# A split-precision encoder layer on one core: TensorE in program order, two weight columns together, weight rests last

## The chip, the core and the metric

The kernel runs on one core of a Trainium2 chip. The metric is the device time of one execution in microseconds (us). TensorE (PE in the profile) multiplies, VectorE (DVE) and ScalarE (ACT) do the elementwise work, GpSimd (POOL) and SyncE (SP) mainly issue transfers. Each engine executes its own instructions in the order in which they stand in its program, and waits on semaphores for the others. The kernel is written with a scheduler: the source gives the operations, and the scheduler chooses the order of each engine's program from what depends on what, priorities and its own estimate of durations, except where the source says otherwise.

## The reference

A residual trunk of two layers over 256 tokens of width 2048, in float32:

```python
for l in range(DEPTH):                      # DEPTH = 2
    h = rms_norm(x, pre_mix_norm[l])
    m = hybrid_mixer(h, l, w_in[l], w_o[l], ...)
    x = x + rms_norm(m, post_mix_norm[l])
    h = rms_norm(x, pre_ffn_norm[l])
    f = (silu(h @ w_gate) * (h @ w_up)) @ w_down
    x = x + rms_norm(f, post_ffn_norm[l])
```

`hybrid_mixer` multiplies `h` by `w_in` (2048 x 6144), feeds eight heads of stick-breaking attention and eight of differential attention with the parts, normalizes each head's output and multiplies by `w_o` (2048 x 2048). The gate and up matrices are 2048 x 5632, the down matrix 5632 x 2048. The weights are 470 MB of reading for two layers with all else, and nearly all of the work is matrix products of 256 tokens with them.

## The kernel before

**Products in three parts.** A float32 operand is split into `hi`, rounded to the form that TensorE multiplies at its full rate, and `lo`, the rest. A product is three matmuls: `sh` with `hi`, `sh` with `lo`, and `sl` with `hi`, where `sh` and `sl` are the rounded form and the rest of the activations, and the stationary operand is a 128 x 128 block of them (128 features by the 128 tokens of one token tile) and the moving operand 128 x 512 of weights. `product` (L1113) issues the three for one bank of PSUM, at L1116, L1117 and L1118. `unit` (L592) does the same for the attention output, at L601 to L603, and `down` (L1353) for the down projection, at L1365, L1366 and L1368.

**Tiles.** 256 tokens are two token tiles (`NT`). 2048 features are 16 tiles of 128 (`KT`), taken two at a time: a pair `kp` of them is one block of weights, 128 partitions x 2 x 512, 512 KB. A stage is a set of columns of 512 weights. Four banks of PSUM hold two columns by two token tiles: in the gate and up stage `c11` and `c12` are gate and up for token tile 0, `c21` and `c22` those for tile 1.

**Weights.** `weight_order` (L77) lays all blocks out in the order of use. SyncE loads each into a `raw` tile (4 of them), ACT rounds it to `hi` (L351), DVE subtracts and writes `lo` (L354); there are six tiles of each, and `feed` (L341) runs four blocks ahead of use (`LOOKAHEAD`). A block's `raw`, `hi` and `lo` come free when the last reader is done.

**Seven products.** For some pairs the 2 x 2 block product (two feature tiles by two columns) is done with seven products instead of eight, from sums of weight blocks (`mixed_weights`, L303: `T` and `G` summed on DVE and POOL, then split into `Th` at L319 and `Tl` at L320) and sums of activations (`token_sums`, L1120, `sh` and `sl`). `seven_products` (L1137) issues them into the four banks and four extra ones, `p1`, `p6`, `p7` and `q5`; `shared_part` combines the extra ones on DVE after the last such pair. In the first gate and up column these are pairs 4 and 6, later more.

**Stages of a layer.** (1) The input projection, six times two columns (`mixer_in`, L980), with the steps of the attention run in between: each call of `tick` (L578) lets waiting parts of the attention issue their next instructions. (2) The output projection: columns 0 and 1 over all pairs, then columns 2 and 3 over `LATE_O` and at the end `LAST_O` = pairs 3 and 7, token tile 0 first for both columns, then tile 1 (L1219 on). `evac_sum` (L614) takes a finished bank out and `rescale` (L626) normalizes: after a chain of small operations (L631 to L636, L508, L509) four instructions of L659 add the scaled columns into `x`. (3) `transposed` (L512) turns 512 columns of `x` at a time on TensorE (L517) into `xT_ps`, and ACT (L520) and DVE (L525) make the rounded form and the rest of the next stage's activations from it (`xF` for the gate and up stage, `xI` for the next layer's input projection), four tiles each time. `inv_rms` (L538) has ACT square all of `x` (L544) for the norm that is applied after the product. (4) Gate and up, eleven columns; in the first one the pairs come as in `FIRST_ORDER` = 0, 1, 3, 2, 7, 4, 6, 5, the first two of them for token tile 0 and then for tile 1. (5) The down projection in two halves of two columns; the last three pairs (`TAIL`) are done column by column within each token tile, so that tile 0 can be rescaled and transposed while tile 1 is still being multiplied. Then the next layer's input projection starts in the same manner as gate and up: two pairs for tile 0, two for tile 1, and the rest.

**What sets the order.** The scheduler orders all engines' programs, PE's too, within what depends on what. `tc.high_priority(offset=URGENT)` lifts some work (evacuation, rescale and, through `then`, tile 1's transposes), `tc.manual_schedule` keeps a block of ACT and DVE work as written (at the end of the output projection), and `tc.issue_after` puts one instruction behind another (`after_rests` and `behind` put sums behind weight rests). Elsewhere PE's order differs from the source locally: where an operand of a seven-product burst is expected late, products of the next pair stand ahead of it.

Of the kernel before, what the change touches and what calls it, by code (L numbers as in the profile page):

```python
# [31 lines left out]
URGENT = 50  # L32
TAIL = 3
# [130 lines left out]
def kernel(  # L164
# [15 lines left out]
    nc = tc.nc  # L180
    const = ctx.enter_context(tc.tile_pool(name="const", bufs=1))
    small = ctx.enter_context(tc.tile_pool(name="small", bufs=4))
    wpool = ctx.enter_context(tc.tile_pool(name="wpool", bufs=1))
    ps = ctx.enter_context(tc.tile_pool(name="ps", bufs=1, space=PSUM))

# [348 lines left out]

    def x_tiles(nm):
        return [x_pool[0].tile([P, 2, S], F32R, tag="xT", bufs=KT, name=f"{nm}_{k}") for k in range(KT)]
# [55 lines left out]
    def unit(accs, stat, i, kp, toks, first, last, ahead=LOOKAHEAD):  # L592
        hi, lo = weights(i, ahead)
        for kk in range(2):
            tick()
            k = 2 * kp + kk
            for t in toks:
                st = stat[k]
                sh, sl = st[:, 0, t * P : (t + 1) * P], st[:, 1, t * P : (t + 1) * P]
                a = accs[t]  # L600
                nc.tensor.matmul(a, sh, hi[:, kk, :], start=first and kk == 0, stop=False, skip_group_check=open_sums[0])  # L601
                nc.tensor.matmul(a, sh, lo[:, kk, :], start=False, stop=False, skip_group_check=open_sums[0])  # L602
                nc.tensor.matmul(a, sl, hi[:, kk, :], start=False, stop=last and kk == 1, skip_group_check=open_sums[0])  # L603
# [22 lines left out]
    def rescale(mg, ssm, t, nm, then=None, newest=None):  # L626
# [11 lines left out]
        if halves:  # L638
# [3 lines left out]
            with tc.issue_after(newest[0].ins):  # L642
                nc.tensor.matmul(xb, ident, first, start=True, stop=False)
# [234 lines left out]

    def opening(pool, accs, xT, stats, sums_of, settle):
# [47 lines left out]
        for kp in range(KT // 2):  # L927
# [3 lines left out]
            if kp + 2 < KT // 2:  # L931
                load()
                fetch(2 * kp + 6)
            for part in ((0,), (1,)) if kp == KT // 2 - 1 else (range(NT),):
                eight_in(accs, xT, 0, PAIRS[0], kp, part, kp == 0, kp == KT // 2 - 1, 0)
# [27 lines left out]
    def eight_in(accs, xT, l, cc, kp, toks, first, last, ahead=LOOKAHEAD):  # L963
        ws = [weights(plan[l]["in"][c, kp], ahead) for c in cc]
        for kk in range(2):
            for t in toks:
                tick()
                st = xT[2 * kp + kk]
                stat = (st[:, 0, t * P : (t + 1) * P], st[:, 1, t * P : (t + 1) * P])
                for col, (hi, lo) in enumerate(ws):  # L970
                    product(accs[2 * t + col], stat, (hi[:, kk, :], lo[:, kk, :]), first and kk == 0, last and kk == 1)
# [8 lines left out]
    def mixer_in(pool, l, rs, xT, mix, mixed):  # L980
# [7 lines left out]
        for n, cc in enumerate(PAIRS):  # L988
# [56 lines left out]
            else:  # L1045
# [3 lines left out]
                for j, kp in enumerate(kps):  # L1049
                    first, last = j == 0, j == len(kps) - 1  # L1050
                    if n == 0 and 2 <= j < 2 + len(IN_SEVEN):
                        sums_of(IN_SEVEN[j - 2])
# [18 lines left out]
                    if n == 0 and j < 2:  # L1071
                        if j == 0:
                            for t in range(NT):
                                for kp in kps[:2]:
                                    eight_in(banks, xT, l, cc, kp, (t,), kp == kps[0], False)
# [34 lines left out]

    open_sums = [False]

    def product(a, stat, moving, first, last):  # L1113
        sh, sl = stat
        hi, lo = moving
        nc.tensor.matmul(a, sh, hi, start=first, stop=False, skip_group_check=open_sums[0])  # L1116
        nc.tensor.matmul(a, sh, lo, start=False, stop=False, skip_group_check=open_sums[0])  # L1117
        nc.tensor.matmul(a, sl, hi, start=False, stop=last, skip_group_check=open_sums[0])  # L1118
# [48 lines left out]
    for l in range(L):  # L1167
# [15 lines left out]
        accs = {(c, t): acc_bank(f"o{l}_{c}_{t}") for c in (0, 1) for t in range(NT)}  # L1183
        forms = {}
        for n, (c, kp) in enumerate(plan[l]["order_o"][:16]):
# [298 lines left out]
```

## Time and profile before

| | |
|---|---|
| median of three runs | 2189.47 us (2189.18 to 2190.63) |
| span of the profiled execution | 2189.2 us |
| TensorE busy | 2174.7 us, 99%, 9980 instructions, granted clock 0.999 |
| weight loads of TensorE busy | 1787.4 us, 82%, 9980 |
| VectorE busy | 1921.7 us, 88%, 2647 instructions |
| ScalarE busy | 1378.0 us, 63% |
| GpSimd busy | 144.2 us, 7% |
| HBM | 470.63 MB read, 223 GB/s over the span |

The profiled execution's own time is within the three runs; its span, from the first to the last instruction, is used as its time below. Rows of the view in order of time begin with the start in us from the start of the span and the duration in us; then come the engine, the line of the kernel, the operation, the output and inputs by name (buffer numbers left out) and their shapes. "x2" joins neighbours of one kind, whose duration is then from the first's start to the last's end. What stands in brackets is how long the engine was idle before and which engine and tile ended that. A duration of a matmul is longer than the step to the next one, since matmuls overlap; steps are read from the starts. Rows of the view of waits give an engine's line, whose result it waited for, the sum of such idle time, how often, and the longest. In the second part of the page each digit is the share in tenths for one fortieth of the span.

### The profile page before, as it was taken

The numbers are of one execution on the slowest core, as the hardware profiler recorded it, in microseconds if no ns is written. First come the engines' busy times: TensorE is split into PE (matmuls) and PEld (weight loads), VectorE is DVE, ScalarE is ACT, GpSimd is POOL, SyncE is SP. The second block draws the span as 40 slices with busy tenths as digits, with TensorE's granted clock in tenths as the row PEclk, the third lists the DMA queues.
The fourth block names the chain that finished last, engine by engine and source line by source line (L and its number), as shares of the span: only waits on it lengthen the run. The fifth ranks groups of instructions, "written<-read, shape, count | busy, mean of one in ns | idle before, by whom it ended". The sixth has DMA issues, their size and how long they took to land.

```text
span 2189.2 us, 28686 instructions
## 1 busy us (share of the span) xinstructions
PE 2174.7 (99%) x9980; PEld 1787.4 (82%) x9980; DVE 1921.7 (88%) x2647; ACT 1378.0 (63%) x2063; POOL 144.2 (7%) x199
## 2 busy tenths in 40 slices
PE   9999999999999999999999999999999999999998
PEld 7888888788888888888878888887788888888886
DVE  7888659999999999989878886699999999999997
ACT  7666665756656666666665656657566566666664
POOL 1100000010010000000010000000000100000000
PEclk9999999999999999999999999999999999999999
DMA  9545577587687786767465555775866877867673
GB/s 322 194 164 173 192 243 267 184 274 234 206 282 235 229 273 210 245 210 257 146 240 173 183 173 183 256 258 195 269 214 226 274 241 232 263 213 234 207 264 101
DMA packets 146033, 489.30 MB, mean 224 GB/s; under 512 B 16592, under 2 KB 17616, under 8 KB 145376
## 3 DMA queue, kind: packets, MB, share of 16 engines
q1 hardware_dynamic: 127712, 450.72, 58.9%
q0 software_dynamic: 17600, 36.22, 8.3%
q8 instruction: 78, 1.28, 0.2%
q10 hardware_dynamic: 576, 0.54, 0.1%
q14 instruction: 67, 0.55, 0.1%
HBM read 470.63 MB, written 16.78 MB: 223 GB/s over the span
## 4 chain that ended last, share of the span: by engine, by line
PE 92%; DVE 5%; ACT 1%; issue 1%; DMA 1%; DVEq 0%; ACTq 0%
PE c L1117 9%; PE c L1118 9%; PE c L1116 9%; PE in L1116 7%; PE in L1118 7%; PE in L1117 7%; PE dn L1368 4%; PE dn L1366 4%; PE dn L1365 4%; PE p L1117 2%; PE p L1118 2%; PE p L1116 2%; PE o L601 2%; PE o L603 2%; PE o L602 2%; DVE lo L354 1%
## 5 line engine op out<-in xcount | busy, mean ns | idle before, releaser
L354 DVE TENSOR_TENSOR lo<-raw,hi 128x1024 fp32r<-128x1024 f32 x514 | 615.2, 1219 | 90.7 <-ACT hi L351 89.8
L351 ACT ACTIVATE hi<-raw 128x1024 fp32r<-128x1024 f32 x514 | 531.3, 1055 | 183.1 <-DMA raw<-in_weights_in_turn_dram 51.3
L1116 PE MATMUL c<-hi,xF 128*128 128x512 f32 x806 | 317.2, 394 | 0.1
L1117 PE MATMUL c<-lo,xF 128*128 128x512 f32 x806 | 314.4, 390 | 1.2 <-DVE lo L354 1.0
L1118 PE MATMUL c<-hi,xF 128*128 128x512 f32 x806 | 314.0, 390 | 0.0
L1117 PEld LDWEIGHTS c<-lo,xF 128*128 128x128 f32 x806 | 151.5, 188 | 33.2 <-DVE lo L354 3.3
L1118 PEld LDWEIGHTS c<-hi,xF 128*128 128x128 f32 x806 | 151.3, 188 | 32.0 <-DVE xF L525 0.4
L1116 PEld LDWEIGHTS c<-hi,xF 128*128 128x128 f32 x806 | 151.4, 188 | 30.3 <-ACT xF L520 0.5
L298 POOL DMA_DIRECT2D T<-in_weights_in_turn_dram x106 | 92.2, 869 | 1257.8 <-DMA T<-in_weights_in_turn_dram 434.6
L1365 PE MATMUL dn<-hi,jh 128*128 128x512 f32 x432 | 168.2, 389 | 0.0
L1366 PE MATMUL dn<-lo,jh 128*128 128x512 f32 x432 | 168.1, 389 | 0.0
L354 DVE TENSOR_TENSOR lo<-G,hi 128x1024 fp32r<-128x1024 f32 x114 | 138.8, 1218 | 21.1 <-ACT hi L351 21.0
L319 ACT ACTIVATE hi<-T 128x1024 fp32r<-128x1024 f32 x114 | 119.7, 1050 | 41.9 <-PE c L1118 23.9
L320 DVE TENSOR_TENSOR lo<-T,hi 128x1024 fp32r<-128x1024 f32 x114 | 138.8, 1217 | 3.2 <-ACT hi L319 2.3
L351 ACT ACTIVATE hi<-G 128x1024 fp32r<-128x1024 f32 x114 | 120.0, 1053 | 30.1 <-PE c L1118 17.4
L319 ACT ACTIVATE Th<-G 128x1024 fp32r<-128x1024 f32 x106 | 111.8, 1055 | 36.8 <-DVE G L335 35.3
L320 DVE TENSOR_TENSOR Tl<-G,Th 128x1024 fp32r<-128x1024 f32 x106 | 129.1, 1218 | 5.5 <-ACT Th L319 5.3
L1368 PE MATMUL dn<-hi,jl 128*128 128x512 f32 x432 | 133.0, 390 | 0.0
L1116 PE MATMUL in<-hi,xT 128*128 128x512 f32 x328 | 131.0, 401 | 1.1 <-ACT hi L921 1.1
L1116 PE MATMUL in<-hi,xI 128*128 128x512 f32 x328 | 131.2, 401 | 0.0
L335 DVE TENSOR_TENSOR G<-G,T 128x1024 f32<-128x1024 f32 x106 | 129.3, 1220 | 1.7
L1117 PE MATMUL in<-lo,xI 128*128 128x512 f32 x328 | 128.1, 390 | 0.3 <-DVE lo L354 0.3
(485 smaller groups left out, 4786.7 us busy)
## 6 DMA issues: line engine op xcount, KB each, us to landing
raw<-in_weights_in_turn_dram SPq DMA_DIRECT2D x514, 512.0 KB, 4.7
G<-in_weights_in_turn_dram SPq DMA_DIRECT2D x114, 512.0 KB, 5.8
T<-in_weights_in_turn_dram SPq DMA_DIRECT2D x106, 512.0 KB, 6.4
T<-in_weights_in_turn_dram POOLq DMA_DIRECT2D x106, 256.0 KB, 7.2
GU<-in_weights_in_turn_dram SPq DMA_DIRECT2D x32, 512.0 KB, 6.5
Gf<-in_weights_in_turn_dram SPq DMA_DIRECT2D x8, 512.0 KB, 6.0
Tf<-in_weights_in_turn_dram SPq DMA_DIRECT2D x8, 512.0 KB, 6.7
V<-in_weights_in_turn_dram SPq DMA_DIRECT2D x8, 512.0 KB, 5.2
```

What stands on the lines that cost most here:

```text
L298: nc.gpsimd.dma_start(sums[i][:, 0, :], stream[i - 1][:, 0, :], accum_op=ALU.add)
L319: nc.scalar.activation(h, w, AF.Copy)
L320: nc.vector.tensor_tensor(out=l, in0=w, in1=h.bitcast(F32), op=ALU.subtract)
L335: nc.vector.tensor_tensor(out=g, in0=g, in1=t2.unsqueeze(1).to_broadcast([P, 2, CW]), op=ALU.add)
L351: nc.scalar.activation(hi, raw, AF.Copy)
L354: rest = nc.vector.tensor_tensor(out=lo, in0=raw, in1=hi.bitcast(F32), op=ALU.subtract)
L1116: nc.tensor.matmul(a, sh, hi, start=first, stop=False, skip_group_check=open_sums[0])
L1117: nc.tensor.matmul(a, sh, lo, start=False, stop=False, skip_group_check=open_sums[0])
L1118: nc.tensor.matmul(a, sl, hi, start=False, stop=last, skip_group_check=open_sums[0])
L1365: nc.tensor.matmul(accs[c, t], sh, hi[:, kk, :], start=first, stop=False, skip_group_check=open_sums[0])
L1366: nc.tensor.matmul(accs[c, t], sh, lo[:, kk, :], start=False, stop=False, skip_group_check=open_sums[0])
L1368: nc.tensor.matmul(accs[c, t], sl, hi[:, kk, :], start=False, stop=last, skip_group_check=open_sums[0])
```

## The change

1. `tc.manual_schedule` for TensorE over the whole kernel: its program is the source's order, exactly.
2. `two_products` replaces two calls of `product`: for both columns first the rest of the activations with `hi`, then the rounded form with `hi`, and last the rounded form with `lo`; the columns alternate. `product` itself has the same new order for one column (`sl` with `hi`, `sh` with `hi`, `sh` with `lo`). One function `eight` does a pair for the input projection, the output projection, gate and up, and down. The output projection, formerly one column after the other within a pair, now takes two columns together, too, and its last pair of columns 0 and 1 one token tile after the other.
3. `first_three`: at the start of the next layer's input projection and of gate and up, the first three pairs (formerly two) go over token tile 0 and then over token tile 1. The transposes of tile 1's columns are put by hand between them: `before` gives, for a number of the twelve groups of six matmuls, the columns that are transposed ahead of it, with a priority lifted by `FIRST` for what follows on ACT and DVE. `rescale` no longer calls `transposed` itself, so the squares of `inv_rms` come ahead of these transposes in the source.
4. The opening's first pair (`first_pair`) has an order of its own: rounded forms with `hi` first for all four banks.
5. The end of the output projection and the last three pairs of the down projection are written in the order in which they are to run: at the end of the output projection tile 0's products of `LAST_O`, then most of tile 1's, with tile 0's transposes ahead of the last ones; in the down projection, tile 0's first two of the last three pairs for both columns together.

Operations, their number and their shapes, and the plan of the weights stay as they were.

```diff
@@ tile_trunk_kernel
+    ctx.enter_context(tc.manual_schedule(engines={mybir.EngineType.PE}))
...
+    def product(a, stat, moving, first, last):
+        sh, sl = stat
+        hi, lo = moving
+        mm(a, sl, hi, first, False)
+        mm(a, sh, hi, False, False)
+        return mm(a, sh, lo, False, last)
+
+    def two_products(banks, stat, ws, kk, first, last, rest_first=True):
+
+        sh, sl = stat
+        his, los = ([w[j][:, kk, :] for w in ws] for j in range(2))
+        jobs = [(sl, his)], [(sh, his), (sh, los)]
+        jobs = jobs[0] + jobs[1] if rest_first else jobs[1] + jobs[0]
+        for n, (st, moving) in enumerate(jobs):
+            for a, w in zip(banks, moving):
+                mm(a, st, w, first and n == 0, last and n == 2)
...
+    def eight(banks, ws, stat, toks, first, last):
+
+        for kk in range(2):
+            for t in toks:
+                tick()
+                two_products(banks[2 * t : 2 * t + 2], stat(kk, t), ws, kk, first and kk == 0, last and kk == 1)
+
+    def first_three(banks, ws, stats, column, before):
+
+        sixes = [(t, j, kk) for t in range(NT) for j in range(3) for kk in range(2)]
+        for n, (t, j, kk) in enumerate(sixes):
+            for at in before.get(n, ()):
+                column(*at)
+            tick()
+            two_products(banks[2 * t : 2 * t + 2], stats[j](kk, t), ws[j], kk, (j, kk) == (0, 0), False)
...
+    def column_of(g0, tiles):
+
+        def column(t, cg):
+            with tc.high_priority(offset=FIRST):
+                transposed(t, g0, tiles, cols=(cg,))
...
@@ output projection, columns 2 and 3
-                for c, i in ((2, i), (3, j)):
-                    unit({t: accs[c, t] for t in range(NT)}, mix, i, kp, range(NT), kp == LATE_O[0], False)
+                ws = [weights(i, LOOKAHEAD), weights(j, LOOKAHEAD)]
+                eight(got, ws, pair_of(mix, kp), (0,) if kp == LATE_O[-1] else range(NT), kp == LATE_O[0], False)
...
+        last_unit(0, 0)
+        eight(got, ws, pair_of(mix, LATE_O[-1]), (1,), False, False)
...
-            rescale(mg, ssm, 1, f"o{l}", lambda t, c: transposed(t, 32 + l * KT, xT, cols=(c,)))
+            rescale(mg, ssm, 1, f"o{l}")
         open_sums[0] = False
         rs = [inv_rms(t, pool, f"ffn{l}") for t in range(NT)]
...
@@ gate and up, first column
             if c == 0:
-                for t in range(NT):
-                    for kp in order[:2]:
-                        eight(banks, c, kp, (t,), kp == order[0], False)
-                order = order[2:]
+                first_three(
+                    banks,
+                    [both(c, kp) for kp in order[:3]],
+                    [pair_of(xT, kp) for kp in order[:3]],
+                    column_of(32 + l * KT, xT),
+                    {6: ((1, 0), (1, 1)), 8: ((1, 2),), 9: ((1, 3),)},
+                )
+                order = order[3:]
...
@@ down projection, last three pairs
+            for kp in range(nkp - tail, nkp):
+                tick()
+                tick()
+                prep(kp)
+                if kp < nkp - 1:
+                    ws = [weights(plan[l]["down"][c, kp], LOOKAHEAD) for c in cc]
+                    eight(got, ws, halves(kp), (0,), False, False)
...
```

183 lines of the change are left out of this document (99 added, 84 removed).

## The prediction

> **What bounds the kernel now.** I read the page's busy shares first, then the costliest groups, then the waits of TensorE, then the order of time around each of these waits.
>
> ```profile
> span 2189.2 us, 28686 instructions
> PE 2174.7 (99%) x9980; PEld 1787.4 (82%) x9980; DVE 1921.7 (88%) x2647; ACT 1378.0 (63%) x2063; POOL 144.2 (7%) x199
> PEclk9999999999999999999999999999999999999999
> L354 DVE TENSOR_TENSOR lo<-raw,hi 128x1024 fp32r<-128x1024 f32 x514 | 615.2, 1219 | 90.7 <-ACT hi L351 89.8
> ```
>
> TensorE (PE) is busy 99% of the span and its clock is full throughout, so the time is the matmuls at their pace plus PE's stalls. VectorE (DVE) is next at 88%: it must split each weight block (`lo`, 514 times) before the third of the products can run. The pace, and whether the order of stationaries matters to it, stand in three rows:
>
> ```profile
> 399.65 0.39 PE L1116 MATMUL c<-hi,xF 128*128 128x512 f32 x1
> 399.88 0.39 PE L1117 MATMUL c<-lo,xF 128*128 128x512 f32 x1
> 400.11 0.39 PE L1118 MATMUL c<-hi,xF 128*128 128x512 f32 x1
> ...
> 1099.56 1.98 PE L517 MATMUL xT_ps<-ident,xd 128*128 128x128 f32 x16 [1.32 <-DVE xd L659]
> 1101.30 0.47 PE L1116 MATMUL in<-hi,xI 128*128 128x512 f32 x1
> ```
>
> L1116 and L1117 use one stationary (`sh`), L1118 another (`sl`); both steps are 0.23 us (0.2267 over long runs of such rows). The 16 transposes take 1.74, 0.109 each. So grouping matmuls with one stationary earns nothing by these rows, and the change can only move stalls. The named ones:
>
> ```profile
> PE xT_ps L517 <- DVE xd L659: 1.3, 1, 1.3
> PE in L1116 <- ACT hi L921: 1.1, 1, 1.1
> PE c L1117 <- DVE lo L354: 1.0, 2, 0.5
> PE p L1117 <- DVE Tl L320: 1.0, 2, 0.5
> ```
>
> Each of these has smaller ones beside it (below). They are where a stage begins or a seven-product burst starts, and all are DVE or ScalarE (ACT) work that arrives late. The median of the three runs, 2189.47 us, is 0.3 above the profiled span of 2189.2; I make the sum against the span and add 0.3.
>
> **The change part by part.** Matmuls, transposes, splits and DMAs are the same in number and shape; what changes is PE's order (now exactly as written) and, through the scheduler, the order on DVE and ACT. I read the three orders off the built program and put the durations of the rows on them.
>
> *Weight rests last.* In a pair of columns `lo` is now needed at the fifth and sixth matmul instead of the second and fifth: 3 steps, 0.7 us later for the first column, 0.2 for the second. A row that waits for `lo` 0.2 to 0.7 us may lose its wait, if DVE's order stays. The price is that the pair starts with the activation's rest `sl`, which is the later of its two halves. In the middle of a stage both are long ready: 0, and if they were not, the same DVE queue would show in the waits.
>
> *Attention output stage, last pairs.*
>
> ```profile
> 380.08 1.28 DVE L1213 TENSOR_TENSOR o<-o,mg_o 128x512 f32<-128x512 f32 x2
> 380.82 0.50 PE L601 MATMUL o<-hi,mix_sb 128*128 128x512 f32 x1
> ```
>
> The columns of token tile 1 now alternate, so the second column's bank, corrected by the second L1213, which ends at 381.36, is needed at the second matmul (381.05), not the seventh: +0.35. The weights of the first column come free three matmuls later, so the next split and, behind it, the tile 0 rescale (L659, below) move 0.76 later (estimate, three steps of 0.23 plus a stop-and-start). Bounds 0 to 0.8.
>
> *FFN start, token tile 0 with three pairs.* The DVE queue:
>
> ```profile
> 391.72 2.74 DVE L659 SCALAR_TENSOR_TENSOR x<-mg_o,tot_o,x 128x512 f32<-128x512 f32 x4
> 395.51 1.12 DVE L525 SCALAR_TENSOR_TENSOR xF<-xT_ps,gains,xF 128x128 fp32r<-128x128 f32 x4
> 400.73 0.22 DVE L508 SCALAR_TENSOR_TENSOR tot_o<-tot_o 128x1 f32<-128x1 f32 x1 [0.43 <-ACT tot_o L635]
> 400.87 1.22 DVE L354 TENSOR_TENSOR lo<-raw,hi 128x1024 fp32r<-128x1024 f32 x1
> 402.33 1.40 DVE L659 SCALAR_TENSOR_TENSOR x<-mg_o,tot_o,x 128x512 f32<-128x512 f32 x2
> 404.44 1.21 DVE L354 TENSOR_TENSOR lo<-raw,hi 128x1024 fp32r<-128x1024 f32 x1
> ```
>
> and PE:
>
> ```profile
> 395.41 0.48 PE L1116 MATMUL c<-hi,xF 128*128 128x512 f32 x1
> 402.14 0.50 PE L1117 MATMUL c<-lo,xF 128*128 128x512 f32 x1 [0.51 <-DVE lo L354]
> 405.28 0.93 PE L1117 MATMUL c<-lo,xF 128*128 128x512 f32 x2
> 415.18 0.39 PE L1116 MATMUL c<-hi,xF 128*128 128x512 f32 x1
> ```
>
> The third pair's rests are the two L354 at 400.87 and 404.44; 402.14 is the matmul that waits for the first. In the changed program's DVE order all four tile 1 rescales (2.65, from the start at 391.72 to 394.37 by the same four) stand ahead of the first rest. So it ends at 400.73 + 0.76 + 0.2 (L508, L509) + 2.65 + 1.15 = 405.5. PE gets there at 395.41 + 0.76 + 0.5 (it now begins with the rest half of `xF`, the first L525 at 395.51) + 28 x 0.227 = 403.0: a stall of 2.5. The second rest comes behind four L525 (4 x 0.26) and its own 1.14, at 407.7: a stall of 1.9 more. From there to the matmul that runs at 415.18 (fourth pair) 43 matmuls (9.75) and 16 transposes (16 x 0.109 = 1.74) are left, and about 0.4 for tile 1's transposes, whose ACT halves now stand behind eight squares (L544): 419.6. That is 4.4 late, the output stage's share in it. Bounds: 5.5, if another 1.1 of DVE split gets in between; below, the waits of before vanish, 0.5 of the named row and as much again in the 405.28 row and around it: -1.4. I take 4.4, since the place in an in-order queue decides it.
>
> *First column, second seven-product burst.*
>
> ```profile
> 432.86 0.39 PE L1116 MATMUL p<-Th,sh 128*128 128x512 f32 x1
> 434.98 1.22 DVE L320 TENSOR_TENSOR Tl<-G,Th 128x1024 fp32r<-128x1024 f32 x1
> 436.12 2.35 DVE L354 TENSOR_TENSOR lo<-raw,hi 128x1024 fp32r<-128x1024 f32 x2
> 436.71 0.39 PE L1117 MATMUL p<-Tl,sh 128*128 128x512 f32 x1
> ```
>
> Before, PE ran the next pair's products while `Tl` was made and took it at 436.71. In program order the third of these products stands two matmuls behind the first (433.3, plus 4.4 = 437.7), and DVE has the two L354 of 436.12 ahead of `Tl`: 438.4, plus what DVE has lost (0.76, and about 1.3 of waiting for tile 1's transposes): about 440.3. Stall 2.6; bounds 0.5 (DVE not late) to 2.6.
>
> *Later bursts.*
>
> ```profile
> 470.32 0.39 PE L1118 MATMUL q<-hi,sl 128*128 128x512 f32 x1
> 470.85 0.73 PE L1116 MATMUL p<-Th,sh 128*128 128x512 f32 x2
> ...
> 472.35 0.39 PE L1118 MATMUL c<-hi,sl 128*128 128x512 f32 x1
> 473.23 0.50 PE L1117 MATMUL p<-Tl,sh 128*128 128x512 f32 x1 [0.50 <-DVE Tl L320]
> ```
>
> ```profile
> 1559.52 0.39 PE L1118 MATMUL q<-hi,sl 128*128 128x512 f32 x1
> 1560.30 0.73 PE L1116 MATMUL p<-Th,sh 128*128 128x512 f32 x2 [0.39 <-ACT Th L319]
> ...
> 1561.80 0.39 PE L1118 MATMUL c<-hi,sl 128*128 128x512 f32 x1
> 1562.68 0.50 PE L1117 MATMUL p<-Tl,sh 128*128 128x512 f32 x1 [0.50 <-DVE Tl L320]
> ```
>
> These steps are over the pace by 0.30 and 0.65, and by 0.55 and 0.65; each wait costs 0.11 more on the matmul behind it (0.34 instead of 0.23). With PE 7.0 late and DVE about 2.1 late they go: 1.2 and 1.4, and with the small ones of the same kind in later columns 1.9 in layer 0 and 2.5 in layer 1. What is late next is a `Tl` that program order wants 1.1 earlier at the second of these bursts (it is a split further back on DVE); it is covered by the same lead, and would cost about 1.2 per layer without it.
>
> *From layer 0 to layer 1.*
>
> ```profile
> 1097.85 0.39 PE L1116 MATMUL in<-hi,xI 128*128 128x512 f32 x1
> 1102.74 0.50 PE L1117 MATMUL in<-lo,xI 128*128 128x512 f32 x1 [0.28 <-DVE lo L354]
> ```
>
> The step from 1097.85 to the transposes of 1099.56 is 1.5 over the pace, and the wait of 1102.74 another 0.45 (with the step before it): 2.3 are lost here with what hangs on them. In the new order one L354 (1.13) stands ahead of the first tile 1 rescale, which is wanted 0.45 earlier: a stall of 1.6 there; three pairs for tile 0 give the other rescales cover, but the third is about 0.8 late, and its restart 0.2. Net +0.3; bounds -2.3 (all hidden) to +1.5.
>
> *Opening and end.*
>
> ```profile
> PE xb_d L646 <- ACT r_d L645: 1.7, 1, 1.7
> ```
>
> The end waits for the scale of the last rows behind the last matmul (this row); the order of its links is kept: 0, bounds -0.2 to +0.4. At the opening the first `hi` (L921 row) is late as before: 0, bounds -0.1 to +0.3. Comparing, over the rest of the program, each matmul's place with the DVE and ACT work ahead of it, I found no operand that loses its cover: 0, bounds -0.5 to +1.2.
>
> Sum: layer 0 4.4 + 2.6 - 1.9 = 5.1; layer 1, whose blocks stand in the same order, 4.4 + 2.6 - 2.5 = 4.5; between them 0.3: 9.9. 2189.2 + 9.9 = 2199.1, and 0.3 for the median: 2199.4.
>
> **A rule against the rows.** A pair of columns used `sh, sh, sl, sh, sh, sl`, where 2 of 6 matmuls follow one with the same stationary; now it uses `sl, sl, sh, sh, sh, sh`, where 4 of 6 do. By row, same and other stationary step alike, and the busy shares count 9980 weight loads for 9980 matmuls, so a load is issued each time: 0. If it did pay, the bound is the part of a step that doesn't hang on the width, 0.227 - 4/3 x (0.227 - 0.109) = 0.070 us, on 9980/3 more matmuls: 233 us, a time of 1957.
>
> [...]
>
> **The rivals.**
>
> *Faster: rests last hide the boundary waits.* If the first weight rest keeps its place ahead of the rescales when it matters (ACT's scale is 0.43 late in the 400.73 row, so DVE may have time), the FFN start gains 1.4 in each layer, no burst is late, and the later bursts (1.9, 2.5) and the layer boundary (2.3) lose their waits; the output stage costs 0.35 twice. -2.8 - 4.4 - 2.3 + 0.7 = -8.8: 2180.7. For it: all named waits are of this kind and short. Against: DVE executes in order, and in the new order 2.65 of rescale stand ahead of that rest. It decides from the point where that rest ends by 403.0.
>
> *No change: lateness paid back.* Only the first rest is late (2.5), the second and tile 1 run inside that, the burst loses 0.5, and the later waits vanish: 2 x 3.0 - 4.4 + 0.3 = +1.9: 2191.4. For it: once PE waits, DVE gains lead on it. Against: DVE has hardly an idle moment there, so what it must do before the fourth pair doesn't shrink.
>
> *Slower still: program order makes PE wait in later bursts as well.* Without the scheduler's deferral the `Tl` of both layers costs 1.2 where I take 1.9 and 2.5 off: +6.8: 2206. It needs DVE's lead of 4.9 to be gone by 472.
>
> *A faster pace* from kept stationaries, as above: down to 1957. That the order does not change at all is excluded by the built program's order.
>
> **Chances and range.** Forecast 0.54, faster 0.20, no change 0.16, slower still 0.08, pace 0.02. A measurement of this kernel tells about 0.2% (4.4 us) from no change. So faster 0.22, same 0.16, slower 0.62. Range 2181 to 2207: it reaches into the faster rival, whose lower half and the pace are left out (0.12), and over the slower one's upper half (0.04). The forecast's own range is 2194 to 2205, from the bounds of the FFN start and the burst.
>
> **What would show it.** In the changed kernel's waits: `c <- DVE lo` near 2.5 and 1.9 us at the first FFN column of each layer, with four rescales ahead of that `lo` on DVE; `p <- DVE Tl` near 2.6 some 35 us later; no `Tl` waits near 473 and 603 us of before's clock; one `xT_ps <- DVE xd` near 1.6 at the layer boundary; steps of 0.227 everywhere else. I am wrong if the first of these waits is under 1 us: then the sign turns, since every other gain remains. If only the burst is right, it ends near 2191.

## The result and the profile after

The changed kernel takes 2230.48 us (median of five runs, 2228.34 to 2235.18), the kernel before 2190.24 (five runs, 2189.18 to 2190.67): a ratio of 1.0188, 95% interval 1.0175 to 1.0200. That is 1.9% slower, clear of the spread, and so slower as forecast, but by 40 us instead of 10, and above the range's end of 2207.

From the page of the changed kernel (parts 1 and 2), and the longest of its waits of TensorE (engine and line, what it waited for, sum in us, times, longest):

```profile
span 2228.1 us, 28795 instructions
PE 2188.9 (98%) x9980; PEld 1796.4 (81%) x9980; DVE 1925.0 (86%) x2647; ACT 1370.4 (62%) x2063; POOL 145.5 (7%) x199
PEclk9999999999999999999999999998999999999999
```

```profile
PE c L191 <- DVE lo L402: 7.7, 4, 2.2
PE c L191 <- DVE xF L573: 4.4, 4, 2.0
PE p L191 <- DVE Tl L368: 4.0, 5, 1.5
PE p L191 <- ACT Th L367: 3.6, 2, 2.1
PE o L191 <- DVE o L1274: 3.5, 2, 1.8
PE xT_ps L565 <- DVE xd L707: 2.6, 2, 1.4
```

All matmuls now stand at one line (L191, `mm`); before's L354 is L402, L320 is L368, L525 is L573, L659 is L707. Where before's waits for `lo` and `Tl` were 0.5 us at the longest, these are 1.5 to 2.2. And the clock row has an 8, in the slice from 1504 to 1560 us, which before's had nowhere; a slice of 56 us averages shorter stretches away. The view by stretches (length, then busy us with the count for PE, PEld, DVE, ACT and POOL, then granted clock, DMA share, GB/s) shows two of them, in layer 0:

```profile
400.00:422.00 22.00, 16.21 (x62) 12.41 (x62) 14.60 (x46) 14.54 (x47) 1.77 (x2) 0.84 0.67 215
440.00:460.00 20.00, 17.30 (x63) 13.18 (x62) 16.47 (x21) 7.58 (x10) 1.76 (x2) 0.83 0.81 258
```

The same view of the kernel before:

```profile
400.00:422.00 22.00, 21.44 (x101) 16.96 (x100) 20.80 (x54) 19.18 (x50) 1.77 (x2) 1.00 0.79 268
```

TensorE is idle for 6 of the 22 us at the gate and up start, and its clock is 0.84 on the mean. DVE, busy for 20.8 of the 22 us before, is now busy for 14.6: it stands idle itself, too. In order of time, TensorE at that place (start, duration, and in brackets the idle time before):

```profile
405.33 1.07 PE L191 MATMUL c<-hi,xF 128*128 128x512 f32 x4
408.56 0.51 PE L191 MATMUL c<-lo,xF 128*128 128x512 f32 x1 [2.17 <-DVE lo L402]
410.73 0.80 PE L191 MATMUL c<-lo,xF 128*128 128x512 f32 x1 [1.66 <-DVE lo L402]
411.33 1.91 PE L191 MATMUL c<-hi,xF 128*128 128x512 f32 x4
413.03 0.93 PE L191 MATMUL c<-lo,xF 128*128 128x512 f32 x2
413.80 1.03 PE L565 MATMUL xT_ps<-ident,x 128*128 128x128 f32 x8
416.79 1.84 PE L191 MATMUL c<-hi,xF 128*128 128x512 f32 x4 [1.96 <-DVE xF L573]
```

The four matmuls at 405.33 take 1.07 us, the four at 411.33 take 1.91: behind the first two waits a step is 0.427 us instead of 0.227 (1.70 over four steps, 411.33 to 413.03). The same sets in behind the third wait.

How late TensorE is against before, from the start of the same stage's first matmul in both traces:

| stage | layer 0 | layer 1 |
|---|---|---|
| output projection, columns 0 and 1 | +1.1 | +22.2 |
| gate and up, first column | +4.3 | +25.4 |
| its fourth pair | +12.5 | +35.5 |
| second column | +18.6 | +40.4 |
| third column | +18.1 | +39.2 |
| down projection | +19.5 | +39.0 |
| input projection of layer 1 / last matmul | +20.8 | +38.9 |

So 17.5 and 18.2 of the 39 us come between the late output projection and the second gate and up column of each layer, where the prediction had put 7.0; nothing is given back later but 0.5 and 1.2 in the second column.

### The profile page after: what moved, and what is told of

The parts are those of the page before. It is cut to its first block, busy times and chain, and to the rows that moved or that the text cites. A ratio compares the mean times of both kernels' runs of the same rounds, so it can differ in the third digit from the quotient of the medians.

```text
span 2228.1 us, 28795 instructions
## 1 busy us (share of the span) xinstructions
PE 2188.9 (98%) x9980; PEld 1796.4 (81%) x9980; DVE 1925.0 (86%) x2647; ACT 1370.4 (62%) x2063; POOL 145.5 (7%) x199
## 5 line engine op out<-in xcount | busy, mean ns | idle before, releaser
L402 DVE TENSOR_TENSOR lo<-raw,hi 128x1024 fp32r<-128x1024 f32 x514 | 615.8, 1220 | 117.2 <-ACT hi L399 102.9
L191 PE MATMUL c<-hi,xF 128*128 128x512 f32 x1612 | 448.0, 396 | 4.4 <-DVE xF L573 4.4
L191 PEld LDWEIGHTS c<-hi,xF 128*128 128x128 f32 x1612 | 302.6, 190 | 66.3 <-DVE xF L573 5.5
L191 PE MATMUL c<-lo,xF 128*128 128x512 f32 x806 | 259.0, 394 | 7.7 <-DVE lo L402 7.7
L191 PEld LDWEIGHTS c<-lo,xF 128*128 128x128 f32 x806 | 152.9, 190 | 41.7 <-DVE lo L402 9.2
L191 PE MATMUL in<-hi,xT 128*128 128x512 f32 x656 | 180.8, 396 | 1.2 <-DVE xT L961 1.2
L191 PE MATMUL in<-hi,xI 128*128 128x512 f32 x656 | 180.7, 396 | 0.0
L402 DVE TENSOR_TENSOR lo<-G,hi 128x1024 fp32r<-128x1024 f32 x114 | 139.1, 1220 | 34.7 <-ACT hi L399 34.4
L191 PE MATMUL dn<-hi,jl 128*128 128x512 f32 x508 | 161.8, 390 | 0.0
L191 PE MATMUL dn<-hi,jh 128*128 128x512 f32 x508 | 161.3, 389 | 0.0
L191 PE MATMUL dn<-lo,jh 128*128 128x512 f32 x508 | 161.3, 389 | 0.0
L368 DVE TENSOR_TENSOR lo<-T,hi 128x1024 fp32r<-128x1024 f32 x114 | 139.0, 1219 | 3.8 <-ACT hi L367 3.8
L191 PEld LDWEIGHTS in<-hi,xT 128*128 128x128 f32 x656 | 120.0, 188 | 27.1 <-issue 2.0
L191 PEld LDWEIGHTS in<-hi,xI 128*128 128x128 f32 x656 | 119.8, 188 | 24.9 <-issue 2.0
L368 DVE TENSOR_TENSOR Tl<-G,Th 128x1024 fp32r<-128x1024 f32 x106 | 129.4, 1221 | 5.1 <-ACT Th L367 4.9
L191 PEld LDWEIGHTS dn<-lo,jh 128*128 128x128 f32 x508 | 95.4, 188 | 19.8
```

The lines of the kernel that those rows point to most:

```text
L191: return nc.tensor.matmul(out, stat, moving, start=start, stop=stop, skip_group_check=open_sums[0])
L368: nc.vector.tensor_tensor(out=l, in0=w, in1=h.bitcast(F32), op=ALU.subtract)
L402: rest = nc.vector.tensor_tensor(out=lo, in0=raw, in1=hi.bitcast(F32), op=ALU.subtract)
```

## The experiments

Theory A: DVE's order at a stage start and program order on TensorE make waits, and half clock follows them. Theory B: program order alone. Theory C: weight rests last. Each kernel was timed against the kernel before on the same chip, whose median was 2189.3 to 2190.2 throughout; the differences below are against 2230.5.

### Undoing one part

**e1.** TensorE left to the scheduler:

```diff
-    ctx.enter_context(tc.manual_schedule(engines={mybir.EngineType.PE}))
```

> The changed kernel with TensorE's order left to the scheduler again; all else of the change stays. Theory A (the time goes where DVE's order puts a rest or a Tl behind other work and program order keeps TensorE from stepping around it, plus half clock after these stalls): the second burst of the first gate and up column has before's DVE order again, so its 5 to 6 us per layer go, the wait for the first weight rest behind the four rescales stays: 2208 to 2218. Theory B (program order alone is the cause): 2188 to 2194. Theory C (weight rests last, held longer, are the cause): 2226 to 2234.

Measured 2209.72 (2208.36 to 2210.61): half of the loss, and inside A's range. But the bursts' loss did not go as A said: TensorE still lost 4.4 and 4.9 us there (e14 shows why).

**e2.** The same line put into the kernel before, nothing else:

> The kernel before with nothing changed but TensorE in program order. Theory A: its source has tile 1's transposes ahead of the whole first gate and up column and p7's third product 3 us ahead of where TensorE ran it, so stalls of 3 us or more at both places in both layers, with half clock behind them: 2205 to 2225. Theory B: 2220 to 2235, the whole loss. Theory C: 2188 to 2193.

Measured 2250.63 (2249.86 to 2251.71), more than any theory said. Waits of this kernel:

```profile
PE xT_ps L518 <- DVE x L660: 25.4, 8, 4.4
PE xT_ps L518 <- DVE xd L660: 10.8, 2, 7.2
PE o L602 <- DVE o L1214: 6.9, 2, 3.6
```

Its source puts each transpose right behind the rescale that feeds it, and in program order TensorE stands there. The scheduler had moved these away. With its hand-written order and the rest of the change, 60 us of loss become 40.

**e3.** The weight rest in the middle again, in the changed kernel (in `product` likewise):

```diff
-    def two_products(..., rest_first=True):
+    def two_products(..., rest_first=False):
```

> The changed kernel with the weight rest in the middle again (sh with hi, sh with lo, sl with hi; columns still alternate). DVE's order at the gate and up start is that of the changed kernel. Theory A: nothing is regained, the waits for lo begin one to two matmuls earlier: 2228 to 2236. Theory C: 2190 to 2200.

Measured 2243.08 (2240.48 to 2245.69): 12.6 slower, more than A said and far from C. Rests last are no part of the loss; in program order they save 12.6.

**e7.** Rests last in the kernel before, scheduled (`product` only, so not the output and the plain down pairs):

```diff
-        nc.tensor.matmul(a, sh, hi, ...); nc.tensor.matmul(a, sh, lo, ...); nc.tensor.matmul(a, sl, hi, ...)
+        nc.tensor.matmul(a, sl, hi, ...); nc.tensor.matmul(a, sh, hi, ...); nc.tensor.matmul(a, sh, lo, ...)
```

> The kernel before with the new order of three products in one column (sl with hi, sh with hi, sh with lo) in the input projection, gate and up, and all seven-product pairs; the scheduler orders TensorE. DVE's order at the gate and up start is that of before. Theory A: no loss, and the short waits for lo and Tl get shorter: 2186 to 2191. Theory C: 2200 or more.

Measured 2204.01 (2201.66 to 2206.04), 14 slower, against A and by its number in C's range. For the larger part of it the trace shows a cause that belongs to neither: 4.1 and 4.9 us are lost at the first bursts of the two layers. The loads of the first bursts' `T` on SyncE's queue, before and then here:

```profile
384.86 21.18 SPq L230 DMA_DIRECT2D raw<-in_weights_in_turn_dram  x6
406.09 0.90 SPq L297 DMA_DIRECT2D T<-in_weights_in_turn_dram  x2
```

```profile
384.86 29.13 SPq L230 DMA_DIRECT2D raw<-in_weights_in_turn_dram  x8
414.04 0.90 SPq L297 DMA_DIRECT2D T<-in_weights_in_turn_dram  x2
```

The scheduler, given other durations of use, put a further `raw` load, which waits for a free tile, ahead of both `T`; they come 8 us later, and TensorE waits for `Th` in the first burst:

```profile
430.88 0.39 PE L1118 MATMUL q<-lo,sh 128*128 128x512 f32 x1
433.43 0.50 PE L1116 MATMUL p<-Th,sl 128*128 128x512 f32 x1 [2.15 <-ACT Th L319]
433.76 0.44 PE L1117 MATMUL p<-Th,sh 128*128 128x512 f32 x1
434.01 0.63 PE L1116 MATMUL p<-Th,sl 128*128 128x512 f32 x1
434.43 0.63 PE L1117 MATMUL p<-Th,sh 128*128 128x512 f32 x1
```

Steps of 0.43 us again, behind one wait of 2.15. The other 5 us are spread over the kernel. So the run doesn't price the order of products by itself: a change of TensorE's order in the source reaches the DMA queue through the scheduler.

### Is the half clock made by the waits?

**e5.** Matmuls of zeros fill the stalls; they add nothing to the bank:

```diff
+    def keep_busy(bank_, n):
+        for _ in range(n):
+            mm(bank_[:, 0:384], zero[:, 0:P], zero, False, False)
```

They stand ahead of the two rests' matmuls (12 and 10), ahead of tile 1's first (12), and in the second burst (9 and 5).

> The changed kernel with matmuls of zeros put into the stalls of the first gate and up column (some 2.0 and 1.7 us ahead of the two rests' matmuls, 2.0 ahead of tile 1's first, 1.5 and 0.9 in the second burst), added to a bank where they change nothing. DVE's and ACT's order is that of the changed kernel. If the half clock follows from TensorE standing idle: the steps of 0.43 us vanish, the operands still arrive when they did, and the time falls by 8 to 12: 2218 to 2223. If the clock falls for another reason (the new order of the matmuls): the slow steps stay and the time is 2229 to 2236.

Measured 2218.83 (2217.36 to 2219.70): 11.7 regained. The same two stretches of layer 0, and TensorE at the gate and up start:

```profile
400.00:422.00 22.00, 21.70 (x110) 15.82 (x111) 17.49 (x51) 17.45 (x56) 1.77 (x2) 1.00 0.71 219
436.00:456.00 20.00, 19.32 (x88) 14.65 (x87) 18.65 (x25) 10.13 (x12) 1.76 (x2) 1.00 0.77 252
```

```profile
406.40 2.12 PE L191 MATMUL c<-zero 128*128 128x384 bf16 x12
408.79 0.50 PE L191 MATMUL c<-lo,xF 128*128 128x512 f32 x1 [0.27 <-DVE lo L410]
409.13 1.80 PE L191 MATMUL c<-zero 128*128 128x384 bf16 x10
410.95 0.50 PE L191 MATMUL c<-lo,xF 128*128 128x512 f32 x1
411.29 1.09 PE L191 MATMUL c<-hi,xF 128*128 128x512 f32 x4
```

The rests arrive no earlier, the clock stays at 1.00 and four matmuls take 1.09: idle time of TensorE lowers its clock. In the changed kernel's trace the steps of 0.427 add up to some 10 us over six stretches, of which this run shows none.

**e8.** Growing waits in mid-stage, with `DEFER_ACT` 6 down to 1 in columns 2 to 7 of layer 0:

> The changed kernel with the transposes of the activations put closer to the end of their column, one tick of six matmuls (1.4 us) closer in each of the columns 2 to 7 of layer 0 (6, 5, 4, 3, 2, 1 ticks instead of 7), so that TensorE waits for the chain of SiLU by growing amounts. If idle time of TensorE lowers its clock: columns with a wait under about 1.5 us keep steps of 0.227 us, and behind waits of more than 2 us there are stretches of 0.43 us steps, some 2 to 5 us long. If the half clock belongs to the place and not to the wait: none in these columns.

The ladder stayed too short to reach the bound: the longest wait in these columns is 1.22 us, and no slow steps follow it, so it tells little (2236.99 in one run):

```profile
759.64 0.66 PE L1387 MATMUL actT_ps<-ident,w 128*128 128x128 f32 x4 [1.22 <-DVE w L1381]
760.05 1.17 PE L191 MATMUL c<-hi,xF 128*128 128x512 f32 x4
```

The other traces give the upper side, and it is no sharp bound. The output projection's wait, 1.76 to 1.91 us and alone, stands 14 times in seven kernels (changed, e3, e4, e5, e8, e9, e10); behind it the clock is halved 5 times and stays full 9 times. In one run, e4's, it does the one in layer 0 and the other in layer 1, as its windows and its TensorE rows at the second place show:

```profile
382.00:390.00 8.00, 6.38 (x27) 5.02 (x28) 5.80 (x8) 2.66 (x3) 0.00 (x0) 1.00 0.64 215
1492.00:1500.00 8.00, 6.13 (x20) 4.49 (x19) 5.01 (x8) 3.02 (x3) 0.00 (x0) 0.79 0.65 226
```

```profile
1494.01 1.56 PE L191 MATMUL o<-hi,mix_sb 128*128 128x512 f32 x4 [1.77 <-DVE o L1274]
1495.41 0.85 PE L191 MATMUL o<-lo,mix_sb 128*128 128x512 f32 x2
1496.06 1.91 PE L191 MATMUL o<-hi,mix_sb 128*128 128x512 f32 x4
```

In layer 0 the row that answers to the last one takes 1.08. Here the slow steps begin 1.6 us behind the wait. The eight waits of 3.9 to 4.4 us in e4, e9, e11 and e13 were all followed by slow steps, and so were the five of 4.1 to 7.2 in e2. Of the 29 waits between, 1.95 to 3.7 us, 27 were, some with a second wait close behind them; one of 3.02 us in e2 (at 396.56) and one of 2.44 in e11 (at 448.76) were not. Nor is 1.8 us a lower end: in e1 a wait of 1.26 us and, 1.4 us later, one of 0.66 at the burst of layer 1 (1533.82) were followed by seven slow steps, and the like pair in layer 0 (434.18) by none. So the same wait has a different outcome at different places, and its length alone doesn't decide; what else does was not varied by any run.

### Where the waits come from

**e4.** The first rest asked for ahead of the four rescales:

```diff
             evac_sum(pool, accs[3, 1], mg, ssm, gpost, 3, 1, f"o{l}", True)
+            feed(idx + 12)
             rescale(mg, ssm, 1, f"o{l}")
```

> The changed kernel with the third pair's splits asked for ahead of tile 1's rescale: on DVE the first rest now stands ahead of the four rescales, the second still behind them. If the place in DVE's order is the cause: the wait of 2.3 us for the first rest goes or falls under 0.8, the second's stays near 2 or grows, the rescales are 1.2 later; net 1 to 3 us per layer and perhaps a shorter stretch of half clock: 2222 to 2228. If DVE's amount of work ahead of tile 1 is the bound whatever its order: within 1.5 us of the changed kernel.

Measured 2230.83 (2229.86 to 2233.00): nothing. The first wait is gone and the second has become 4.3:

```profile
410.60 0.79 PE L191 MATMUL c<-lo,xF 128*128 128x512 f32 x1 [4.26 <-DVE lo L402]
```

So it is DVE's work up to the second rest, whichever rest comes first, that sets this point.

**e9.** Tile 1's first transposes ahead of the waiting matmuls:

```diff
-                    {6: ((1, 0), (1, 1)), 8: ((1, 2),), 9: ((1, 3),)},
+                    {4: ((1, 0), (1, 1)), 7: ((1, 2),), 9: ((1, 3),)},
```

> The changed kernel with tile 1's first two transposes of the gate and up start two groups earlier, ahead of the matmuls that wait for the third pair's rests, and its third one group earlier. The scheduler then also puts the eight splits of tile 1's activations ahead of the second rest on DVE, and one rest fewer ahead of Tl in the burst. Theory A (transpose, eight ACT instructions and a DVE one stand uncovered between tile 0 and tile 1 in program order: the 2.2 us wait for xF): that wait goes, the wait for the second rest grows to about 4, one stretch of half clock remains instead of two; the burst's wait falls to 1 to 2. 5 to 10 us are regained: 2220 to 2225. If ACT and DVE are simply full there, the order does not matter: within 2 us of the changed kernel.

Measured 2216.17 (2214.14 to 2216.89): 14.3 regained by the places of twelve transposes in each layer. In the changed kernel the third wait above is a chain that nothing covers:

```profile
413.80 1.03 PE L565 MATMUL xT_ps<-ident,x 128*128 128x128 f32 x8
...
414.44 2.17 ACT L568 ACTIVATE xF<-xT_ps,gains 128x128 fp32r<-128x128 f32 x8 [1.91 <-PE xT_ps L565]
...
416.38 2.16 DVE L573 SCALAR_TENSOR_TENSOR xF<-xT_ps,gains,xF 128x128 fp32r<-128x128 f32 x8 [3.41 <-ACT xF L568]
```

Eight transposes, eight ACT instructions, then the first of DVE, while DVE stands idle for 3.4 us. Turned earlier, DVE does these splits ahead of the second rest, the third wait is gone, the first two are 0.9 and 3.9, and in the burst one of 0.44 is left:

```profile
408.18 0.50 PE L191 MATMUL c<-lo,xF 128*128 128x512 f32 x1 [0.88 <-DVE lo L402]
412.57 0.79 PE L191 MATMUL c<-lo,xF 128*128 128x512 f32 x1 [3.89 <-DVE lo L402]
```

But only a third of the gain lies at this place. By TensorE's lateness in the two traces, 1.8 and 3.6 us are regained at the gate and up starts of the two layers, and 5.4 and 4.2 at the second bursts behind them: there DVE starts the burst's last `Tl` at 442.90 instead of 447.93, with fewer rests ahead of it. How much of this comes from the idle time that DVE no longer has, and how much from its changed order, the run doesn't separate.

**e10.** No weights asked for ahead in the first column's two bursts:

```diff
-            hi, lo = weights(plan[l]["gate"][c, kp], LOOKAHEAD)
-            m = weights(plan[l]["up"][c, kp], LOOKAHEAD)
+            ahead = 0 if c == 0 else LOOKAHEAD
+            hi, lo = weights(plan[l]["gate"][c, kp], ahead)
+            m = weights(plan[l]["up"][c, kp], ahead)
```

> The changed kernel with no weights asked for ahead during the two bursts of the first gate and up column, which puts the four next rests behind the second burst's G and Tl on DVE (all else as it is). Theory A (the burst's loss is those rests ahead of G and Tl): the waits of 2.2 and 1.0 us (1.7 and 1.7 in layer 1) and the half clock behind them go, the next pair's rests come late instead by less than 1 us: 4 to 6 us per layer regained: 2218 to 2223. If the burst is late for another reason (its T and G loaded late): within 2 us of the changed kernel.

Measured 2237.04 (2232.33 to 2238.30), 6.6 worse (the profiled run, the fastest, 2.5). The burst runs through, and the wait stands in the next pair:

```profile
453.21 0.79 PE L191 MATMUL c<-lo,xF 128*128 128x512 f32 x1 [2.43 <-DVE lo L402]
454.34 0.80 PE L191 MATMUL c<-lo,xF 128*128 128x512 f32 x1 [0.34 <-DVE lo L402]
```

Here DVE's order only chooses where TensorE waits.

**e6.** Columns 0 and 1 of the output projection one after the other:

```diff
-            ws = [weights(plan[l]["o"][c, kp], LOOKAHEAD) for c in (0, 1)]
-            for toks in ...: eight(got, ws, pair_of(mix, kp), toks, ...)
+            for c in (0, 1):
+                hi, lo = weights(plan[l]["o"][c, kp], LOOKAHEAD)
+                for kk in range(2):
+                    for t in range(NT):
+                        product(got[2 * t + c], pair_of(mix, kp)(kk, t), (hi[:, kk, :], lo[:, kk, :]), ...)
```

> The changed kernel with columns 0 and 1 of the output projection one after the other within a pair again (new order of the three products kept). If the two weight blocks of a pair, both held to the pair's end, are what makes ACT and DVE late there (DVE is 3.0 us late at the end of that stage while TensorE is 1.1 late): DVE is under 1.5 late, the wait of 1.9 us for the corrected bank falls under 0.8, and 2 to 4 us per layer are regained: 2222 to 2227. If not: within 1.5 us of the changed kernel.

Measured 2223.19 (2222.90 to 2227.10): 7.3 regained, and 2.7 between the two profiled runs, of which this one's is the slowest of its kernel. The wait for the corrected bank is gone, which is 2.2 and 2.3 us at the output projections of the two layers. DVE at the same work, changed kernel and then by column:

```profile
329.91 2.36 DVE L402 TENSOR_TENSOR lo<-raw,hi 128x1024 fp32r<-128x1024 f32 x2 [3.56 <-ACT hi L399]
...
383.05 1.29 DVE L1274 TENSOR_TENSOR o<-o,mg_o 128x512 f32<-128x512 f32 x2
```

```profile
327.01 1.22 DVE L402 TENSOR_TENSOR lo<-raw,hi 128x1024 fp32r<-128x1024 f32 x1 [0.55 <-ACT hi L399]
...
381.66 1.29 DVE L1277 TENSOR_TENSOR o<-o,mg_o 128x512 f32<-128x512 f32 x2
```

Before, the corrections stood at 380.08. In pairs, two blocks come free at once, and DVE waits 3.6 us for its next `hi` and then has two rests to do; it carries this lateness to the corrections. DVE is 1.6 late there instead of 3.0. The edit also takes back the order of the stage's last pair, one token tile after the other; the run doesn't separate the two.

### Do the mends add up?

**e11, e12.** The edits of e4, e6, e9 and e10 together; the same with e1's line out:

> The changed kernel with four mends together: output projection by column, the first rest ahead of tile 1's rescale, tile 1's transposes earlier, no weights ahead in the first bursts. TensorE stays in program order. If the stalls named so far and the half clock behind them are the whole loss: what is left is the opening and the attention (about +1), the later columns (+1 to 2) and the layer boundary (+1 to 2), so 2192 to 2204. If program order costs something that is spread over the whole kernel: 2210 or more.

> The same four mends with TensorE left to the scheduler. If the rest of the change (pairs of columns, rests last, three pairs a token tile) is itself neutral once these places are mended: 2186 to 2195, and it may end below the kernel before. If the change's order of the products costs of itself: 2198 to 2210.

Measured 2220.53 (2219.55 to 2221.24) and 2201.53 (2201.24 to 2202.90). The first missed because two of the four do nothing or harm; the second time lies where the order of the products would cost of itself, which e14 doesn't bear out.

**e13, e15.** Only e6 and e9, which regained something; and with zeros in the two waits that are left at the gate and up start:

> The changed kernel with the two mends that regained time: tile 1's transposes earlier in the gate and up start, and columns 0 and 1 of the output projection one after the other. If they act on different stalls, their gains in the spans add: 14 to 16 from the first, 2.5 to 3.5 from the second, 2209 to 2213. If the output stage's lateness only shifts the wait of the next stage, the second brings nothing: 2214 to 2217.

> The two mends, and matmuls of zeros in the 1 and 4 us waits for the third pair's rests in the gate and up start. If the half clock there comes from the idle time: no steps of 0.43 us behind these waits, 3 to 4 us less than with the two mends alone: 2205 to 2210. If it does not: within 1 us of it.

Measured 2210.31 (2208.72 to 2213.16) and 2206.66 (2205.29 to 2207.16), both as expected: the mends add, and the half clock behind these waits is worth 3.7. Of the 19 us that e13's trace is still behind before's, some 7 in each layer arise between the end of the output projection and the fourth pair of gate and up.

**e14, e16.** The edits of e1 and e6; and with `ahead = 2` at e10's place:

> The changed kernel with TensorE left to the scheduler and the output projection by column. Beside the run with four mends it asks for weights ahead in the bursts as ever: if that was what cost 5 us in the second column there, 2192 to 2197; and if pairs of columns with rests last are of use once TensorE's order is free, 2186 to 2191. If the bursts' loss of 4 to 5 us a layer comes back: 2198 to 2206.

> As the run before in this list, with two blocks asked for ahead instead of four in the first column's bursts. If the amount of DVE work between the bursts and the next column is the bound, the wait lies either in the first column's second burst or in the next pair, and the time is within 2 us of the run with four ahead; if the order counts: 3 to 6 us less.

These two, TensorE scheduled, by column, with four and with two blocks ahead, measured 2195.22 (2194.69 to 2196.89) and 2194.98 (2192.27 to 2197.01), ratios 1.0026 (1.0016 to 1.0035) and 1.0023 (1.0013 to 1.0032). Against e12, which differs in e4's and e9's edits as well as in not asking ahead, e14 regains 6.3 us. By the traces 3.1 and 3.3 us arise from the first column's bursts to the second column in the two layers, where not asking ahead acts, so it is likely its price; e12's three edits weren't tried singly there.

e14 differs from e1 in the output projection alone, and that is worth most of what e1 had left: e1 is 19.6 us behind the kernel before, e14 5.0. DVE's corrections in e1 and in e14:

```profile
383.04 1.29 DVE L1273 TENSOR_TENSOR o<-o,mg_o 128x512 f32<-128x512 f32 x2
```

```profile
379.66 1.29 DVE L1276 TENSOR_TENSOR o<-o,mg_o 128x512 f32<-128x512 f32 x2
```

With DVE 3.4 us earlier there, the 4.4 and 4.9 us that e1 lost at the bursts become 0 and 0.6: they were the output projection's lateness carried on. So the pair of columns in the output projection is dear (14.5 us here, 7.3 under program order in e6), and the other pairs of columns, rests last and three pairs a token tile together are nearly neutral when the scheduler places TensorE's work; no kernel here beats the one before.

## Why the prediction was wrong

**Right: the pace.** Steps of 0.227 us stand in the changed kernel wherever its clock is full, with a stationary kept or not, the opening's ten bf16 matmuls apart (512 columns each, 3.71 us together; 4.24 before). The change moved only stalls, and with them the clock.

**Right: the two waits for rests.** The step had the tile 1 rescales ahead of the rest and stalls of 2.5 and 1.9 us. Measured as time over the pace, 2.33 and 1.94 (the rows show 2.17 and 1.66 idle). But the cause, "the place in an in-order queue", was half of it: put ahead, the same time appeared at the second rest (e4).

**Rests last, put at 0.** Under program order, putting the rest back into the middle costs 12.6 (e3), so this part of the change saves time there; what it is worth with TensorE scheduled, no run shows.

**Failed: "about 0.4 for tile 1's transposes".** The time over the pace there is 2.20 and 2.27. I let the chain run beside tile 0's matmuls; in program order the transposes stand behind all of them, and eight ACT instructions and one of DVE lie bare. Moving them (e9) brought back 14.3 with what hangs on them, most of it at the second burst. The prediction's "DVE has hardly an idle moment there" holds for before's trace (20.8 of 22 us) and not for the changed kernel's (14.6), where DVE waits for this chain.

**Failed: no price for the clock.** No term of the sum and no rival had it. Before's granted clock was full, with waits of up to 0.5 at the gate and up starts and the bursts and one of 1.3 at the layer boundary, and my own stalls of 2.5 and 1.9 in a row lay beyond what that trace showed. It is the largest miss: 11.7 by e5. Behind such waits a step of 512 columns took 0.427 us instead of 0.227, over six stretches of the changed kernel's trace. What length of wait does it the runs don't settle: 1.77 us alone did it in layer 1 of e4 and not in layer 0, and 3.02 in e2 did not.

**Failed in size: the output projection, 0.35 to 0.8.** It lost 3.2 in each layer. I priced the order of the last matmuls and took DVE's time from before's trace; DVE itself was 3.0 late there, from the two columns being taken together (e6, e14).

**Failed in size: the second burst, 2.6, and what follows.** Its waits, as time over the pace, were 2.25 for `Th` and 1.01 for `Tl` in layer 0, 1.64 and 1.68 in layer 1, and slow steps behind them: 6.1 and 4.9 in all. I had looked at `Tl` alone; `Th` comes late as well, since `G` stands behind two rests on DVE. And "order decides" was again too simple (e10): what regained time there was DVE coming out of the stages before it earlier (e9, e14).

**Failed: the gain of 1.9 and 2.5 in later bursts.** 0.5 and 1.2 came back; a wait of 0.76 for `Tl` stands in the second column where I had none. That DVE had no lead of 4.9 there, since TensorE's waits were DVE's own lateness and no head start for it, is my reading and wasn't tried by itself.

**Layer boundary and elsewhere.** Net +0.3 was forecast; 3.4 us of waits stand there against 2.3 before, +1.1, inside the bounds. Two waits in the attention stages (0.9 and 0.75 in layer 0) and an opening that is 0.5 shorter make the +1.1 before the output projection, near the bound of 1.2 for the rest of the program.

The rivals fared so: "faster" fell with the first wait, which came as forecast; "no change" fell with the second one and with tile 1's late start; "slower still" had the right side and the wrong mechanism.

## What to carry to other kernels

On an engine that is 99% busy, an order written by hand is only as good as the cover that it leaves over each chain to another engine and back: look, for every producer on the busy engine (here the transposes), at what stands between it and its consumer. Where the busy engine waits for all of DVE's work up to a point, a changed order of that work only moved the wait (e4, e10). What regained time was taking away a chain during which DVE itself stood idle (e9), and letting DVE reach the stage earlier, by taking one column of weights after the other in the stage before (e6, e14). So count its work and its idle time up to the point, not its queue place, and follow lateness from one stage into the next. And a forecast of waits on TensorE has to price the clock behind them: after waits of about 1.8 us it was halved 5 times in 14, from 3.9 us on each time.

## What the runs showed of the hardware

Idle time of 1.76 to 1.91 us on TensorE, alone, halved its clock in 5 places of 14, idle time of 1.95 to 3.7 in 27 of 29, and of 3.9 to 7.2 in 13 of 13, and a pair of 1.26 and 0.66 close together in 1 of 2: steps of 512 columns go from 0.227 to 0.427 us for about 2 to 6 us, beginning up to some 2 us behind the wait. Matmuls of zeros in the gap keep the full clock (1.00 in e5, where the changed kernel had 0.84 and 0.83). Ten of them, 384 bf16 columns each, take 1.82 us there (409.13 to 410.95), 0.47 ns a column; the rounded form's 512 columns take 0.227 us, 0.44 ns a column. Five runs of the changed kernel spread over 0.3%, with mean clocks of 0.990 to 0.993, where the kernel before spreads over 0.07%; that this is where the slow stretches happen to begin is likely, and wasn't tried by itself.
